# Moving one block sum and one group of quarter sums in a seven-product matmul's VectorE queue

## The chip, the cores and the metric

The kernel runs on one core of a Trainium2 chip. The metric is the device time of one execution in microseconds (us): 1536.24 us is the median of three runs of the kernel before (1536.0 to 1539.86). The engines are TensorE (PE; its weight loads are shown as PEld), VectorE (DVE), ScalarE (ACT), GpSimd (POOL) and SyncE (SP). SP, ACT and POOL issue the DMAs; here SP and ACT issue plain ones, and POOL those that also round float32 to float16.

## The reference

```python
def reference(a, b, alpha):          # a, b: 4096 x 4096 float32, alpha: 0.01
    x = np.matmul(a, b)
    return np.where(x > 0, x, alpha * x)
```

## The kernel before

The output is made in regions of 1024 x 1024, in four groups of four: a group `g` has 1024 rows of A, a region of it one set of 1024 columns of B. The very first region is computed plainly; the list `regions` holds the other fifteen. Each of these is a product of 2 x 2 blocks (A by 2 x 2 blocks of 512 rows and 2048 of K, B by 2 x 2 blocks of 2048 of K and 512 columns), and it is made with seven block products in place of eight. Every block of A or B is held as two units `k` of eight chunks of 128. All operands are float16, the accumulators are eight PSUM banks.

The sums of A's blocks are s1 = a21 + a22, s2 = s1 - a11, s3 = a11 - a21 and s4 = a12 - s2; they are made once in a group. Those of B's blocks are made in every region, in place: t3 = b22 - b12 over b12, t2 = b11 + t3 over b11, b21 - t2 over b21, and last t1 = b22 - t2 over t2. The seven products, `product(0)` to `product(6)` (L792, L652), are called first to seventh here: a11 b11, a12 b21, s2 t2, s3 t3, s1 t1, a22 (b21 - t2) and s4 b22. A whole one is 64 matmuls of 512 columns.

From the second group on, some of these products are themselves split once more in the same manner, into 2 x 2 quarters and seven quarter products of 16 matmuls of 256 columns (`quarter_product`, L745). Such a product needs four quarter sums of its A operand (`sums_of_a`, L692, with the sums at L700 and a DMA that keeps each in DRAM at L701; or `sums_of_s3`, L724) and its quarters of B (`t3_of_b` L680, `sums_of_b` with t2, t4 and t1 at L686, L688 and L690). There are three sorts of regions in a group from the second on:

- The **first region** of a group (`first_of_group`). Its sixth and seventh products are in quarters (`sixth_in_quarters` L843, `seventh_in_quarters` L892). It makes the quarter sums of s4 and of a22 and keeps them in DRAM for the group's other regions. The sums of a22 are used at once by its sixth product; those of s4 are read back from DRAM by ACT's queue during the sixth product (L860).
- The **second and third regions**, and in the last group the fourth too (`in_fourth`): the fourth product is in quarters as well (`fourth_in_quarters` L817). There are seven such regions.
- The **turning region**, the last one of a group but the final one, in which the next group's A is brought in. The change does not reach it.

The order of work is written out by hand: every engine runs its instructions in the order of the program, and only semaphores hold it back. So a place in the code is a place in the engine's queue. What stands in DVE's queue around the change, before:

1. In a first region, beside the third product (s2 t2): the adds of the second product's banks (L967), two leaky ReLUs (L312), b21 - t2 for two units (L588, called at L1084), the four quarter sums of s4 (L700, called at L1091), then t1 for two units (L588, called at L1109), the four quarter sums of a22 (L700, called at L1114), t3, t2, t4 and t1 of the sixth product's quarters of B (L680 to L690), t3 of the seventh's (L680), `add_v` (L972), and then the adds of the sixth product (L967 and, in `more`, L856). The sixth product's quarter products take turns on four PSUM banks: its fourth one and its sixth one add into a bank that DVE must have read before.
2. In an `in_fourth` region, beside the third product: t3, t2 and t4 of the fourth product's quarters, b21 - t2 for two units (L1084), t1 of the fourth product's quarters (L690, called at L1103), t1 of B's blocks for two units (L1109), then the adds of the fourth product's parts (L1124). The fourth product needs its t1 for its sixth quarter product.

Two buffer pools matter. `a16` has three buffers; each call of `new_a16` (L762) takes the next, and the first instruction that writes it waits until the last reader of its former content is done, a DMA out of it included. `x` has three large ones; its tile `q` (`t`, L1100) has four quarters and takes the place of s2, which is free when the third product has been issued and read. The rooms of the quarter sums before: s4's four in four `a16` buffers, a22's first three in three more, a22's fourth in `t[:, 3]`. The quarters `t[:, 0]` to `t[:, 2]` are used by the sixth product's sums of B (L1134).

`keep_x21` (L714) sends a quarter of the A operand itself to DRAM on SP's queue. POOL's queue fetches the next region's B with `fetch_b` (L507, the DMAs at L532): 512 KB each, four of them for each block, and each waits until the products have read the buffer that it fills.

Of the kernel before, what the change touches and what calls it, by code (L numbers as in the profile page):

```python
# [16 lines left out]
SUB = mybir.AluOpType.subtract  # L17
# [30 lines left out]
def kernel(  # L48
# [292 lines left out]
    for what, i, *more in order:  # L341
        if what == "a":
            r, tiles = more
            k = slice(r * rw, (r + 1) * rw)
# [106 lines left out]
    for i in range(1, len(steps)):  # L451
        t, h, u, first, last = steps[i]
# [19 lines left out]
        t, h, u, first, last = steps[i]  # L472
# [93 lines left out]
    def sum_a(g, name):  # L566
        blk = lambda h, half, k: at[g, h, 2 * half + k]
        if name != "s3" and (g, name, 0) not in s:
            new_s(g, name)
        for k in range(2):  # L570
            if name == "s1":
                a_sum(s[g, "s1", k], blk(1, 0, k), blk(1, 1, k), ADD)
            elif name == "s2":
                a_sum(s[g, "s2", k], s[g, "s1", k], blk(0, 0, k), SUB)
            elif name == "s3":
                s[g, "s3", k] = blk(1, 0, k)
                a_sum(s[g, "s3", k], blk(0, 0, k), blk(1, 0, k), SUB)
            else:
                a_sum(s[g, "s4", k], blk(0, 1, k), s[g, "s2", k], SUB)
# [6 lines left out]
    def b_sum(to, x0, x1, op):  # L586
        f = lambda t: t.rearrange("p c n -> p (c n)")
        nc.vector.tensor_tensor(f(to), f(x0), f(x1), op)  # L588
# [79 lines left out]
    def b_quarter(t):  # L668
        return t.rearrange("p (c n) -> p c n", n=HALF)

    def quarters_of_b(i, half, nt):
        return {(k, n): have_b[i, 2 * half + k, nt][:, :, n * HALF:(n + 1) * HALF]
                for k in range(2) for n in range(2)}

    def quarters_of_a(g, name):
        return {(h, k): operand(g, name, k)[:, :, h * HALF:(h + 1) * HALF, :] for h in range(2) for k in range(2)}
# [5 lines left out]
    def sums_of_b(y, to, some=(2, 4, 1)):  # L682
        tt = nc.vector.tensor_tensor
        f = lambda n: b_quarter(to[n])
        if 2 in some:
            tt(f(2), y[0, 1], y[0, 0], ADD)  # L686
        if 4 in some:
            tt(f(4), y[1, 0], f(2), SUB)  # L688
        if 1 in some:
            tt(f(1), y[1, 1], f(2), SUB)  # L690

    def sums_of_a(g, name, room):  # L692

        x = {key: q.rearrange("p c m e -> p c (m e)") for key, q in quarters_of_a(g, name).items()}
        made = {}

        def make(n, x0, x1, op):
            made[n] = room(n)
            f = lambda t: made[t].rearrange("p (c m) -> p c m", m=2 * HALF) if isinstance(t, int) else x[t]
            nc.vector.tensor_tensor(f(n), f(x0), f(x1), op)  # L700
            nc.sync.dma_start(kept_q[name][n - 1], made[n])  # L701

        make(1, (1, 0), (1, 1), ADD)
        make(2, 1, (0, 0), SUB)
        make(3, (0, 0), (1, 0), SUB)
        make(4, (0, 1), 2, SUB)

    def x21(g, name):
        return operand(g, name, 0)[:, :, HALF:, :]

    def by_chunk(t):
        return t.rearrange("p c m e -> p c (m e)") if len(t.shape) == 4 else t.rearrange("p (c m) -> p c m", m=2 * HALF)

    def keep_x21(g, name):  # L714
        if g < G - 1:
            nc.sync.dma_start(by_chunk(kept_x21[name]), by_chunk(x21(g, name)))
# [45 lines left out]
    def new_a16(_=None):  # L762
        return a16_pool.tile([P, QUARTER], DT, name="q16", tag="a16")
# [18 lines left out]
    for i, (g, j) in enumerate(regions):  # L782

        ks = (1, 0) if in_quarters else (0, 1)
# [3 lines left out]
        B = lambda half, nt, k: have_b[i, 2 * half + k, nt]  # L788
# [204 lines left out]
        def fetch_a(h, half, n):  # L993
            if n == 0:
                coming["rows", h, half] = small_pool.tile([P, 16], FP32, name="rows", tag=f"rows{half}")
            coming[h, half][n][0]()
# [21 lines left out]
        first_of_group = i == 0 or regions[i - 1][0] != g  # L1018
        in_quarters = g > 0 and not turning
        in_fourth = in_quarters and not first_of_group  # L1020
# [15 lines left out]
        if have_t2:  # L1036
            for k in ks:
                t = have_b[i, k, 0] = b_pool.tile([P, KC, NT], DT, name="b", tag="b11")
# [41 lines left out]
                    nc.sync.dma_start(kept_last[k, nt], B(1, nt, k).rearrange("p c n -> p (c n)"))  # L1080
        if i == 0:
            sum_a(g, "s4")
        for k in ks:
            b_sum(B(1, 0, k), B(1, 0, k), B(0, 0, k), SUB)  # L1084
        if turning and g:
            t3_of_b(quarters_of_b(i, 0, 1))
            for n in range(3):
                fetch_a(0, 1, n)
        if first_of_group and g:
            keep_x21(g, "s4")  # L1090
            sums_of_a(g, "s4", new_a16)  # L1091
        if not g:
            bring_a(0, 1)

# [4 lines left out]
        if g:  # L1099
            t = x_pool.tile([P, 4, QUARTER], DT, name="q", tag="x")  # L1100
        if in_fourth:
            tq[1] = t[:, 3]
            sums_of_b(quarters_of_b(i, 0, 1), tq, (1,))  # L1103
        elif turning and g:
            tq, sx4 = {2: t[:, 0], 4: t[:, 1], 1: t[:, 2]}, t[:, 3]
            sums_of_b(quarters_of_b(i, 0, 1), tq, (2, 4, 1))
            nc.sync.dma_start(sx4, kept_s3)
        for k in ks:
            b_sum(B(0, 0, k), B(1, 1, k), B(0, 0, k), SUB)  # L1109
        if late_ones:  # L1110
            late_ones[0].end()
        if in_quarters and first_of_group:
            sq = {4: t[:, 3]}
            sums_of_a(g, "a22", lambda n: sq.setdefault(n, sq[4] if n == 4 else new_a16()))  # L1114
            keep_x21(g, "a22")
# [106 lines left out]
    with tc.If(even == 0):  # L1222
        for m in range(M // RM):
            a_blocks = []
            for u in range(KU):
                t = a_pool.tile([P, KC // 2, RM, 2], BF16, name="a", tag=f"a{u // 2 + 1}{m % 2 + 1}")
# [6 lines left out]
            for n in range(N // NT):  # L1233
                banks = [new_bank(n % 2 * 4 + mt) for mt in range(MT)]
                cols = slice(n * NT, (n + 1) * NT)
                for u in range(KU):
                    t = b_pool.tile([P, KC, NT], BF16, name="b", tag=f"b{u // 2 + 1}{n % 2 + 1}")
# [8 lines left out]
                for mt in range(MT):  # L1246
                    t = c_pool.tile([P, 2, NT], FP32, name="c", tag=f"c{side}")[:, 0]
# [44 lines left out]
```

## Time and profile before

| what | value |
|---|---|
| median of three runs | 1536.24 us |
| the profiled execution's own time | 1538.0 us |
| its span, first to last instruction | 1535.8 us |
| PE busy | 1523.6 us (99% of the span) |
| DVE busy | 1158.6 us (75%) |
| ACT, POOL busy | 426.2 us (28%), 281.8 us (18%) |
| granted TensorE clock, mean | 0.999 |
| HBM | 361.76 MB read, 106.43 MB written |

The page names for each group of instructions the line, the engine, the tiles written and read, the count, the busy time, the mean of one in ns, and the idle time before them with what ended it. The timeline lists the instructions of an engine in order of time: start, length, line, operation, tiles, count and, in brackets, the idle time before and who ended it. A DMA is listed where it is issued; its time to landing runs from there to the last of its semaphore's updates. Matmuls are pipelined, so a row of 64 whole ones is shown as 13.98 us, while the next row starts 13.81 us after it; 16 quarter ones are shown as 1.91 us and follow each other by 1.75 us.

The first regions of groups two, three and four span about 411 to 508, 787 to 880 and 1160 to 1253 us; the seven `in_fourth` regions follow them.

### The profile page before, as it was taken

What the parts mean: (1) busy time and instruction counts of PE and PEld (TensorE: products, weight loads), DVE (VectorE), ACT (ScalarE), POOL (GpSimd) and SP (SyncE); (2) the same over time, 40 slices, a digit from 0 to 9 for tenths busy, and PEclk for the clock granted to TensorE, in tenths of its full rate; (3) what the DMA queues carried; (4) which work ended last, traced back from release to release, by engine and by line L of the source; (5) the groups of instructions that cost most, each with busy time, mean ns of one, the idle gap of its engine ahead of it and who ended that gap; (6) DMA issues with size and microseconds to landing.
All of it is one profiled execution on the core that took longest, in us unless ns stands there. A gap on an engine that the chain in (4) does not pass through costs nothing. (4 is left out here: it accounts for less than half of the span.)

```text
span 1535.8 us, 21827 instructions
## 1 busy us (share of the span) xinstructions
PE 1523.6 (99%) x8667; PEld 846.6 (55%) x8667; DVE 1158.6 (75%) x1207; ACT 426.2 (28%) x730; POOL 281.8 (18%) x458
## 2 busy tenths in 40 slices
PE   9999999999999999999999999999999999999998
PEld 4444444444445567574544747557554475746656
DVE  4368867765698686768769798686976968788497
ACT  2201344646310312103551031312464103041220
POOL 5641110143202011022220201110331110101100
PEclk9999999999999999999999999999999999999999
DMA  9999895998879979599798989959899895948934
GB/s 243 186 215 205 235 279 172 180 194 174 226 281 276 259 171 273 135 290 263 163 269 276 289 190 204 277 148 327 169 231 286 238 280 143 275 169 193 279 128 140
DMA packets 205442, 342.87 MB, mean 223 GB/s; under 512 B 18833, under 2 KB 148113, under 8 KB 195346
## 3 DMA queue, kind: packets, MB, share of 16 engines
q0 software_dynamic: 136704, 129.00, 52.7%
q1 hardware_dynamic: 62002, 186.81, 33.1%
q10 hardware_dynamic: 6624, 25.56, 4.4%
q8 instruction: 70, 1.15, 0.3%
q14 instruction: 42, 0.34, 0.1%
HBM read 361.76 MB, written 106.43 MB: 305 GB/s over the span
## 5 line engine op out<-in xcount | busy, mean ns | idle before, releaser
L801 PE MATMUL ps<-b,a 128*128 128x512 f16 x2624 | 570.9, 379 | 0.1
L801 PE MATMUL ps<-b,s 128*128 128x512 f16 x2240 | 489.2, 379 | 1.0 <-ACT c L814 1.0
L801 PEld LDWEIGHTS <-a 128*128 128x128 f16 x2624 | 256.8, 98 | 308.1 <-issue 0.6
L801 PEld LDWEIGHTS <-s 128*128 128x128 f16 x2240 | 219.0, 98 | 263.8 <-DVE b L588 1.5
L588 DVE TENSOR_TENSOR b<-b 128x4096 f16<-128x4096 f16 x104 | 235.1, 2289 | 66.7 <-DMA b<-in_b_dram 62.1
L532 POOL DMA_DIRECT2D b<-in_b_dram x160 | 118.5, 746 | 862.2 <-PE ps L751 325.2
L814 ACT COPY c<-ps 128x512 f32<-128x512 f32 x164 | 84.6, 596 | 444.9 <-PE ps L801 401.1
L141 DVE STREAM_TRANSPOSE a<-a 128x512 uint32<-128x512 uint32 (+2 forms) x120 | 127.0, 1106 | 101.4 <-DMA a<-in_a_dram 101.2
L132 POOL DMA_DIRECT2D a<-in_a_dram x252 | 137.3, 551 | 267.9 <-ACT junk L607 101.4
L751 PEld LDWEIGHTS <-q 128*128 128x128 f16 x1424 | 139.3, 98 | 17.8 <-issue 1.7
L607 ACT ACTIVATE junk<-a 128x512 bf16<-128x512 f16 x192 | 121.1, 631 | 99.6 <-DMA a<-in_a_dram 94.4
L312 DVE SCALAR_TENSOR_TENSOR c<-c 128x1024 f32<-128x1024 f32 (+2 forms) x123 | 141.8, 1195 | 3.9 <-ACT c L814 3.7
L230 ACT ACTIVATE sq<-b 128x2048 bf16<-128x2048 f16 x64 | 119.2, 1910 | 59.5 <-DVE sq L239 42.0
L751 PEld LDWEIGHTS <-a 128*128 128x128 f16 x1200 | 117.3, 98 | 18.7 <-DVE q L690 1.1
L967 DVE TENSOR_TENSOR c<-ps,c 128x512 f32<-128x512 f32 x140 | 87.5, 683 | 43.6 <-PE ps L801 42.0
L282 PE MATMUL ps<-b,a 128*128 128x512 f16 x512 | 112.4, 379 | 0.7 <-ACT a L379 0.2
L751 PE MATMUL ps<-b,q 128*128 128x256 f16 x784 | 91.9, 273 | 1.0 <-DVE c L856 1.0
L751 PE MATMUL ps<-b,a 128*128 128x256 f16 x752 | 88.3, 273 | 0.0
L282 PEld LDWEIGHTS <-a 128*128 128x128 f16 x512 | 49.6, 98 | 61.3 <-issue 1.7
L903 ACT COPY c<-ps 128x512 f32<-128x512 f32 x9 | 5.3, 586 | 272.0 <-PE ps L751 120.2
L751 PEld LDWEIGHTS <-s 128*128 128x128 f16 x624 | 61.1, 98 | 7.1
L856 DVE TENSOR_TENSOR c<-ps,c 128x512 f32<-128x512 f32 x80 | 52.3, 686 | 13.7 <-PE ps L751 13.7
(104 smaller groups left out, 903.7 us busy)
## 6 DMA issues: line engine op xcount, KB each, us to landing
b<-in_b_dram POOLq DMA_DIRECT2D x168, 512.0 KB, 13.9
out_dram<-c SPq DMA_DIRECT2D x240, 256.0 KB, 5.8
a<-in_a_dram POOLq DMA_DIRECT2D x244, 128.0 KB, 5.7
b<-kept SPq DMA_DIRECT2D x20, 1024.0 KB, 9.3
q<-kept_qs ACTq DMA_DIRECT2D x40, 512.0 KB, 7.9
s<-kept_s SPq DMA_DIRECT2D x18, 1024.0 KB, 7.4
q<-kept_qa SPq DMA_DIRECT2D x28, 512.0 KB, 7.5
b<-kept_last SPq DMA_DIRECT2D x12, 1024.0 KB, 11.5
```

Source lines behind the costliest of these rows:

```text
L132: nc.gpsimd.dma_start(a16[32 * q:32 * q + 32], src.rearrange("(g i) w -> i g w", i=32))
L141: nc.vector.transpose(part.rearrange("p c m e -> p c (m e)").bitcast(U32) .rearrange("p c (g i) -> p g c i", i=32), src[:, :, i * n:(i + 1 ...
L230: nc.scalar.activation(to, self.parts[n], SQUARE)
L282: nc.tensor.matmul(ps, a_cols(at[0, h, u], c, mt, (h, u) == (0, 0)), bt[0, u, nt][:, c, :], start=first, stop=last,)
L312: nc.vector.scalar_tensor_tensor(t, t, alpha, t, op0=MULT, op1=MAX if alpha <= 1 else MIN)
L532: nc.gpsimd.dma_start(t[:, c:c + 4, :], b_rows(j, u, c, 4, nt, g > 0))
L588: nc.vector.tensor_tensor(f(to), f(x0), f(x1), op)
L607: nc.scalar.activation(junk, piece[:, q, :], SQUARE, accum_out=to[:, 4 * n + q:4 * n + q + 1])
L751: nc.tensor.matmul(to[m], xq[:, c // 2, rows, c % 2], yq[:, c, :], start=first and c == 0 and m < banks, stop=c == KC - 1, skip_group_chec ...
L801: nc.tensor.matmul(banks[mt], a_cols(t, c, mt, t is first_a), B(half, nt, k)[:, c, :], start=first and (k, c) == todo[0], stop=(k, c) == t ...
L814: nc.scalar.copy(kept[mt], banks[mt])
L967: nc.vector.tensor_add(to, bank, to)
```

## The change

In the seven `in_fourth` regions, only the first unit of b21 - t2 stays in its place; the second is issued behind t1 of the fourth product's quarters. In the three first regions, the keeping of s4's quarter and the four quarter sums of s4 are issued behind t1 of B's blocks, directly ahead of a22's quarter sums, and the rooms change: s4's first three sums go to `t[:, 0]` to `t[:, 2]`, its fourth to an `a16` buffer. The number of instructions and of DMAs stays the same.

```diff
         if i == 0:
             sum_a(g, "s4")
-        for k in ks:
+        for k in ks[:1] if in_fourth else ks:
             b_sum(B(1, 0, k), B(1, 0, k), B(0, 0, k), SUB)
         if turning and g:
             t3_of_b(quarters_of_b(i, 0, 1))
             for n in range(3):
                 fetch_a(0, 1, n)
-        if first_of_group and g:
-            keep_x21(g, "s4")
-            sums_of_a(g, "s4", new_a16)
         if not g:
             bring_a(0, 1)
...
         if in_fourth:
             tq[1] = t[:, 3]
             sums_of_b(quarters_of_b(i, 0, 1), tq, (1,))
+            b_sum(B(1, 0, ks[1]), B(1, 0, ks[1]), B(0, 0, ks[1]), SUB)
         elif turning and g:
...
         if in_quarters and first_of_group:
+            keep_x21(g, "s4")
+            sums_of_a(g, "s4", lambda n: t[:, n - 1] if n < 4 else new_a16())
             sq = {4: t[:, 3]}
             sums_of_a(g, "a22", lambda n: sq.setdefault(n, sq[4] if n == 4 else new_a16()))
             keep_x21(g, "a22")
```

## The prediction

> **What bounds the kernel.** I read the list of waits first, for PE, since the page gives PE 1523.6 us busy of 1535.8 and a granted clock of 0.999: what a reordering can win lies in the 12.2 us between the two, and only where PE waits. Three of its seven rows lie near the change:
>
> ```profile
> PE ps L751 <- DVE c L856: 1.3, 2, 1.0
> PE ps L801 <- ACT c L814: 1.0, 1, 1.0
> PE ps L751 <- DVE q L690: 0.8, 1, 0.8
> ```
>
> (line, waited for: us in total, times, longest.) PE's timeline gives the places of these four waits. Three waits are in group two's first region: ahead of the fifth product, and ahead of the fourth and the sixth quarter product of the sixth.
>
> ```profile
> 467.99 13.99 PE L801 MATMUL ps<-b,s 128*128 128x512 f16 x64 [0.99 <-ACT c L814]
> ...
> 487.57 1.91 PE L751 MATMUL ps<-q,q 128*128 128x256 f16 x16 [0.36 <-DVE c L856]
> ...
> 492.23 1.91 PE L751 MATMUL ps<-b,q 128*128 128x256 f16 x16 [0.96 <-DVE c L856]
> ```
>
> One more, 0.78 us at 1304.56, is in group four's second region. The first regions of groups three and four have none. The ACT copy named at 467.99 is not what PE needs there: the weight loads' row names DVE b L588 for 1.5 us, and that is t1.
>
> Then DVE's timeline in that region, around the change:
>
> ```profile
> 459.43 1.23 DVE L700 TENSOR_TENSOR q<-s 128x2048 f16<-128x2048 f16 x1
> 460.69 1.23 DVE L700 TENSOR_TENSOR q<-q,s 128x2048 f16<-128x2048 f16 x1
> 461.83 1.22 DVE L700 TENSOR_TENSOR q<-s 128x2048 f16<-128x2048 f16 x1
> 464.50 1.23 DVE L700 TENSOR_TENSOR q<-s,q 128x2048 f16<-128x2048 f16 x1 [1.45 <-DMA kept_qs<-q]
> 465.64 4.49 DVE L588 TENSOR_TENSOR b<-b 128x4096 f16<-128x4096 f16 x2
> 471.14 1.23 DVE L700 TENSOR_TENSOR q<-a,a 128x2048 f16<-128x2048 f16 x1 [1.01 <-DMA kept_qs<-q]
> 473.14 1.23 DVE L700 TENSOR_TENSOR q<-q,a 128x2048 f16<-128x2048 f16 x1 [0.78 <-DMA kept_qs<-q]
> 475.17 1.22 DVE L700 TENSOR_TENSOR q<-a 128x2048 f16<-128x2048 f16 x1 [0.80 <-DMA kept_qs<-q]
> 476.31 1.22 DVE L700 TENSOR_TENSOR q<-a,q 128x2048 f16<-128x2048 f16 x1
> ```
>
> The reader is to see two things: t1 (L588) stands behind s4's four sums, and four of the eight quarter sums wait, 4.04 us together, until an `a16` buffer has left for DRAM. From 475.17 on DVE works without a gap until 492.18, and PE's two waits in the sixth product hang on that chain. So in this region DVE is the bound.
>
> **Part two, the `in_fourth` regions.** One L588 unit (2.29 us busy, 2.2 us from start to start) moves behind L690. In group four's second region:
>
> ```profile
> 1298.88 4.49 DVE L588 TENSOR_TENSOR b<-b 128x4096 f16<-128x4096 f16 x2
> 1303.28 1.22 DVE L690 TENSOR_TENSOR q<-b,q 128x2048 f16<-128x2048 f16 x1
> ...
> 1304.56 1.92 PE L751 MATMUL ps<-q,a 128*128 128x256 f16 x16 [0.78 <-DVE q L690]
> ```
>
> The quarter product before began at 1301.87, so PE could have begun this one at 1301.87 + 1.75 = 1303.62; it lost 0.94 us. L690 now starts at 1301.1 and ends at 1302.3: the wait goes, **-0.94**. What is late next is t1 of B's blocks, whose place in the queue does not change: its first unit ends at about 1306.7 and the fifth product would come at 1308.07 - 0.94 = 1307.13. It holds, by 0.4 us. In two other regions (641.52 and 1014.13) L690 waits until PE has read s2, for 1.38 and 0.62 us, and the moved unit now stands behind that wait: t1 ends up to 2.2 us later, at 649.3 and 1021.9. The fifth product reads its second unit from about 660.5 and 1033.1, so this is hidden by the rest of the fourth product; without that cover it would be 2 us each. In the other four nothing waits. Nothing here issues a DMA.
>
> **Part one, the three first regions.** It adds no instruction. It moves t1 by four sums ahead (465.64 to 459.43 in group two), so the stall at 467.99 goes: 467.99 against 453.01 + 13.81 = 466.82, that is 1.17 us. It takes three of s4's sums out of `a16`, so six small waits go (4.04 us here, and 0.37 and 0.42 us in groups three and four). SP's queue holds the same DMAs in the same order, since nothing of it lies between the two places.
>
> But it adds one wait. `a16` has three buffers. s4's fourth sum takes one, a22's first and second the others, and a22's third needs the one of s4's fourth, which must have **landed** in DRAM. Before, t1 (4.4 us) and two more sums lay between the two; now only two sums, 2.3 us. Behind the waiting sum all of DVE's queue stands: a22's fourth, the sixth product's t3, t2, t4, t1, `add_v`, and the adds that let PE go on. So the cost hangs on L, the time from the issue of that write to its landing.
>
> DVE's new times, by the row pitches above (two L588 4.40, four quarter sums 3.54 from first start to last, the last 1.23 long):
>
> - Group two: t1 459.43, s4's sums from 463.83, the fourth ends 468.60.
> - Group three: from the row of b21 - t2 at 826.72: t1 831.12, s4 835.52, the fourth ends 840.29.
> - Group four: from 1199.47: t1 1203.87, s4 1208.27, the fourth ends 1213.04.
>
> a22's third sum then starts at that end + L. From its start to PE's sixth quarter product the gapless chain takes 492.23 - 475.17 = 17.06 us. PE by itself, without any wait, would reach that quarter product at 466.82 + 13.81 + 5 x 1.745 = 489.36 in group two; in groups three and four it reached it at 862.98 + 1.745 = 864.73 and 1235.98 + 1.745 = 1237.73. So:
>
> - Group two: change = 468.60 + L + 17.06 - 492.23 = L - 6.57, not below 489.36 - 492.23 = -2.87.
> - Group three: 840.29 + L + 17.06 - 864.73 = L - 7.38, not below 0.
> - Group four: 1213.04 + L + 17.06 - 1237.73 = L - 7.63, not below 0.
>
> **What L is.** The trace has these very writes (512 KB, 128 x 4 KB) at other places; DMA to landing, least, median and most: s4's four in groups two and three, a22's four in groups three and four.
>
> ```profile
> DMA to landing us min/median/max: 3.7/9.1/10.0
> ...
> DMA to landing us min/median/max: 2.6/2.8/5.6
> ...
> DMA to landing us min/median/max: 8.5/9.3/10.3
> ...
> DMA to landing us min/median/max: 6.0/6.6/10.0
> ```
>
> Alone a write takes 2.6 to 2.8 us. Beside POOL's loads of the next region's B, which begin at 460.38, 835.73 and 1208.73, the last of four in a row takes 9.4 to 10.3 (in groups three and four that is a22's last, issued 3.5 us after the first); only where sums were themselves held up and came 1.1 to 2.0 us apart (a22 in group two) was it 6.1 to 7.0. Before, three of s4's four writes in groups three and four were out ahead of the loads, and none now is (first issues about 465.1, 836.8, 1209.5). Bounds: 3.7 (a first write beside a load) and 10.3. I take 9.5 in groups three and four, where the writes stand to the loads as s4's did in group two before (10.0 the third, 9.4 the fourth, by the sum that waited for it), and 8.2 in group two, between its own two rows, since there the first two loads have run 4.6 us by then.
>
> The Trainium skill (DMA: Bandwidth & Descriptors, "Queues, rings and completion order") says that each DMA engine takes turns between queues packet by packet. From 468 to 473 us SP's queue moved 340 packets and POOL's 356, so the trace agrees; by that alone four writes of 128 packets at 68 a us take 7.5 us from their first packet, L would be near 7, and the sum about -0.5 us.
>
> **Sum:** 8.2 - 6.57 = +1.6, 9.5 - 7.38 = +2.1, 9.5 - 7.63 = +1.9, and -0.9 from part two: **+4.7 us**. All four are on PE's path, since PE has no other wait after them that could swallow them. At both ends of L: 3.7 gives -2.9 - 0.9 = -3.8, and 10.3 gives 3.7 + 2.9 + 2.7 - 0.9 = +8.4. The sum is made against the span of 1535.8 us; the profiled execution took 1538.0, 2.2 us of it outside the span, and the median of the runs is 0.4 above the span. I add to the median: 1536.24 + 4.7 = **1540.9 us**.
>
> **Rivals.**
>
> 1. *Not slower: the writes land soon enough.* One mechanism: the end of s4's fourth write. It decides at L = 7.4: there the sum is +0.8 + 0 + 0 - 0.9, about zero. For it: a22's 6.1 to 7.0 in group two, and s4's fourth in groups three and four, 5.6 and 4.8, partly beside a load. Against: the 9.4 to 10.3 of every write that was last of four beside loads. At L = 6 it gives -0.6 - 0.9 = -1.5, 1534.7 us; at best -3.8, 1532.5 us. The Trainium skill (same page, "Anatomy of one DMA") gives 2.0 us + bytes / 436e3, that is an estimate of 3.2 us for 512 KB. By that this rival would hold, at its best; the rows alone agree with it, those beside loads do not.
> 2. *Slower still: the loads pay too.* The writes leave a stretch of idle DMA engines (before the loads begin) for a full one, so each write moved costs the loads behind it about 1.3 us. In group two's second region t2's first unit is ready at 534.79 for a third product at 535.58, 0.8 us of room. With L at 10.3 and one such miss of 1 us: +9.4, 1545.6 us. Against it: PE itself comes later by then.
> 3. *The change doesn't do what it says.* If L690 was not what PE waited for at 1304.56, part two gives nothing: +5.6, 1541.8 us. PE starts 0.1 us after its end, which speaks against this.
>
> **How the numbers follow.** About 0.3% (4.6 us) is what a measurement of this kernel can tell from no change. Forecast (L of 8 to 10, +1.4 to +7.5): 0.6; rival one 0.25; rival two 0.1; rival three 0.05. Of the forecast a little over half lies above 4.6 us, so slower is 0.32 + 0.1 + 0.04 = 0.46; faster would need more than the -3.8 of the best end, 0.03; the rest, 0.51, is within. The range leaves out the best end of rival one and the last of rival two: 1534.7 to 1545.
>
> **What would show it.** In the changed trace: no wait at the fifth product in group two and none at L690 in group four's second region; of the six small waits of L700 one left in each first region, on `kept_qs`, of L - 2.3, some 6 to 7 us, at a22's third sum; DVE c L856 ahead of the sixth product's fourth and sixth quarter products in all three first regions. L below 7 in the rows of these writes, or a22's third sum in another buffer, would make the forecast wrong.

## The result and the profile after

| | before | after |
|---|---|---|
| median of 22 runs each | 1536.05 us | 1543.12 us |
| lowest and highest | 1533.49 to 1541.61 | 1539.87 to 1546.64 |
| profiled execution, own time | 1538.0 | 1542.66 |
| its span | 1535.8 | 1540.8 |
| ratio of the times | | 1.0048, 95% interval 1.0041 to 1.0055 |

The change makes the kernel slower by 7.1 us by the medians. The two profiled executions differ by 5.0 us of span; the one of before lies 2.0 us above its median, the one of after 0.5 us below, which makes up most of the rest. What follows about places is read from these 5.0 us.

PE's rows of the list of waits of the changed kernel (line, waited for: us in total, times, longest):

```profile
PE ps L751 <- DVE c L856: 5.0, 4, 1.5
PE ps L751 <- DVE q L690: 2.3, 1, 2.3
...
PE ps L801 <- DVE b L588: 0.4, 1, 0.4
PE ps L801 <- DMA b<-in_b_dram: 0.4, 1, 0.4
PE ps L751 <- DVE q L734: 0.4, 1, 0.4
```

The 1.0 us at the fifth product is gone. The adds of the sixth product (L856) cost 5.0 us in place of 1.3, and the 2.3 us on L690 is a new wait at another place than the old 0.8. DVE's timeline of the changed kernel in group two's first region shows where they come from:

```profile
463.01 1.22 DVE L700 TENSOR_TENSOR q<-s 128x2048 f16<-128x2048 f16 x1
...
466.54 1.22 DVE L700 TENSOR_TENSOR q<-s,q 128x2048 f16<-128x2048 f16 x1
467.68 1.22 DVE L700 TENSOR_TENSOR q<-a,a 128x2048 f16<-128x2048 f16 x1
468.93 1.23 DVE L700 TENSOR_TENSOR q<-q,a 128x2048 f16<-128x2048 f16 x1
476.73 1.23 DVE L700 TENSOR_TENSOR q<-a 128x2048 f16<-128x2048 f16 x1 [6.58 <-DMA kept_qs<-q]
```

The small waits between the sums are gone, and one large one stands ahead of a22's third sum, until s4's fourth write has landed. Groups three and four have the same wait, of 6.36 and 8.05 us. Behind it PE is late. PE's timeline of the changed kernel, group two and then group four:

```profile
465.87 13.98 PE L801 MATMUL ps<-b,s 128*128 128x512 f16 x64
...
483.94 1.92 PE L751 MATMUL ps<-q,q 128*128 128x256 f16 x16 [2.35 <-DVE q L690]
...
489.13 1.91 PE L751 MATMUL ps<-q,q 128*128 128x256 f16 x16 [1.53 <-DVE c L856]
...
493.80 1.91 PE L751 MATMUL ps<-b,q 128*128 128x256 f16 x16 [0.96 <-DVE c L856]
...
1238.34 1.91 PE L751 MATMUL ps<-q,q 128*128 128x256 f16 x16 [1.53 <-DVE c L856]
...
1243.01 1.91 PE L751 MATMUL ps<-b,q 128*128 128x256 f16 x16 [0.96 <-DVE c L856]
```

The fifth product begins at 465.87 in place of 467.99, and the sixth quarter product at 493.80 in place of 492.23, so a lead of 2.1 us is lost again, with 1.6 on top. Of this lead 1.2 us is the stall that is gone, and 0.95 us was there already at the product ahead of it (452.06 in place of 453.01), which the change does not touch. In group four the sixth quarter product comes at 1243.01 in place of 1237.73. Followed instruction by instruction, PE's lag behind the kernel before goes like this:

| stretch | change of PE's lag |
|---|---|
| start of the kernel, not touched by the change | -0.9 |
| group two: 1.2 won at the fifth product, 3.7 lost in the sixth | +2.5 |
| group three, first region | 0 |
| group three, second region (two waits, one of them for a load) | +1.05 |
| group four, first region | +2.8 |
| group four, second region, a wait on L734 | +0.6 |
| there, t1 of the fourth product (part two) | -0.9 |
| small steps elsewhere | -0.1 |
| sum | +5.0 |

### The profile page after: what moved, and what is told of

It is laid out like the page before. It is cut to its first block, busy times and chain, and to the rows that moved or that the text cites. A ratio compares the mean times of both kernels' runs of the same rounds, so it can differ in the third digit from the quotient of the medians.

```text
span 1540.8 us, 21831 instructions
## 1 busy us (share of the span) xinstructions
PE 1523.7 (99%) x8667; PEld 846.6 (55%) x8667; DVE 1157.4 (75%) x1207; ACT 426.4 (28%) x730; POOL 281.9 (18%) x458
## 5 line engine op out<-in xcount | busy, mean ns | idle before, releaser
L588 DVE TENSOR_TENSOR b<-b 128x4096 f16<-128x4096 f16 x104 | 234.8, 2289 | 64.5 <-DMA b<-in_b_dram 60.7
L967 DVE TENSOR_TENSOR c<-ps,c 128x512 f32<-128x512 f32 x140 | 87.5, 682 | 37.9 <-PE ps L801 24.7
L751 PE MATMUL ps<-q,q 128*128 128x256 f16 x480 | 57.3, 273 | 5.4 <-DVE c L856 3.1
```

The lines of the kernel that those rows point to most:

```text
L751: nc.tensor.matmul(to[m], xq[:, c // 2, rows, c % 2], yq[:, c, :], start=first and c == 0 and m < banks, stop=c == KC - 1, skip_group_chec ...
L967: nc.vector.tensor_add(to, bank, to)
```

## The experiments

Each kernel was run beside the kernel before on the same chip; ratios are against it. The experiments were run in three batches on three chips, so kernels of different batches are compared by their ratios.

**The two parts alone.** In the first kernel part two is undone, in the second part one.

```diff
-        for k in ks[:1] if in_fourth else ks:        # part1_alone
+        for k in ks:
-            b_sum(B(1, 0, ks[1]), B(1, 0, ks[1]), B(0, 0, ks[1]), SUB)
```

> Part one without part two (the second unit of b21 - t2 back ahead of t1 of the fourth product's quarters). The theory (the wait of a22's third sum for the write of s4's fourth costs the time; part two takes away one stall of 0.94 us): the changed kernel's +7.1 plus 0.9, some +8.0 us against the kernel before, and the stall ahead of the quarter product that needs L690 in group four's second region is back. The rival that part two is what costs: about 0 to -1 us.

> Part two without part one (s4's quarter sums back ahead of t1, in four a16 buffers). The theory: -0.9 us against the kernel before, with no wait of PE in group four's second region, and t1 of B's blocks some 2.2 us later in two regions without anyone waiting for it. The rival that part two costs or does nothing: 0 or above.

Part one alone: 1543.68 us, ratio 1.0066 (1.0053 to 1.0079). Part two alone: 1534.24 us, 0.9997 (0.9988 to 1.0006). The loss is all in part one. Part two wins its 0.99 us at the quarter product behind L690 in the trace of its own kernel, but no difference shows in the time.

This trace shows one thing more. Up to group two's first region the kernel of part two alone has the same instructions as the kernel before, and yet the stalls that the prediction read there are not in it. PE's timeline, from the product ahead of the fifth to the next region, with every wait of that stretch:

```profile
454.50 13.98 PE L801 MATMUL ps<-b,a 128*128 128x512 f16 x64
468.31 13.98 PE L801 MATMUL ps<-b,s 128*128 128x512 f16 x64
...
508.95 26.06 PE L801 MATMUL ps<-b,a 128*128 128x512 f16 x120 [0.48 <-DMA b<-in_b_dram]
```

PE came 1.5 us later to 454.50 than in the kernel before, by differences in the first 95 us, and DVE's sums waited 1.8 us for their buffers in place of 4.0. Of the three stalls in the profiled execution of before, 2.9 us together, none is left. So how much PE stalls there differs from one execution to the next by as much as the change could win there.

**The wait taken away.** In this kernel, early_room, a22's third sum gets an `a16` buffer that held s4's first sum, not its fourth.

```diff
-            sums_of_a(g, "s4", lambda n: t[:, n - 1] if n < 4 else new_a16())
+            sums_of_a(g, "s4", lambda n: new_a16() if n == 1 else t[:, {2: 0, 3: 2, 4: 1}[n]])
```

> The changed kernel with one edit: of s4's quarter sums the first takes the a16 buffer, and the second, third and fourth take t's quarters 0, 2 and 1. a22's third sum then waits for the write of s4's first sum, issued 3.5 us earlier and ahead of three others. All instructions and DMAs stay where they are. The theory (the wait on the buffer sets the time): the wait falls from 6.4 to 8.1 us to 0 in groups two and three and to 2.3 or less in group four, and PE's waits in the sixth products go: -2.9 in group two and 0 in group four, less 0.9 by part two, plus up to 2 us of late loads in group three's second region: -1 to -4 us against the kernel before. The rival (the writes, moved beside POOL's loads, cost the time by making those late): it moves the same writes, so it stays at +4 or more.

It came out at 1544.92 us, ratio 1.0076 (1.0063 to 1.0089): slower than before by 10 us, and not faster by 1 to 4. The wait did go, as DVE's timeline of this kernel shows:

```profile
468.82 1.22 DVE L700 TENSOR_TENSOR q<-q,a 128x2048 f16<-128x2048 f16 x1
469.96 1.22 DVE L700 TENSOR_TENSOR q<-a 128x2048 f16<-128x2048 f16 x1
```

PE reaches the sixth quarter product of group two's sixth product at 488.45, 3.8 us ahead of the kernel before; 0.9 of this is from the start of the kernel. Then PE waits for something else. The waits of this kernel, and PE's timeline in the next region:

```profile
PE ps L801 <- DMA b<-in_b_dram: 6.5, 3, 3.8
PE ps L751 <- DVE q L734: 2.1, 1, 2.1
```

```profile
505.70 1.89 PE L801 MATMUL ps<-b,a 128*128 128x512 f16 x8 [1.36 <-DMA b<-in_b_dram]
511.35 4.87 PE L801 MATMUL ps<-b,a 128*128 128x512 f16 x14 [3.77 <-DMA b<-in_b_dram]
```

The 3.8 us in hand turn into a lag of 1.7 us, and of 3.4 by the next product (538.94 in place of 535.58; see the last section). Waits of 0.6 to 1.0 us for writes of s4, ahead of single sums of B's quarters, are left in DVE's queue. So the theory that the wait of a22's third sum is all that the change costs, and that without it the change wins, falls.

**Another order with a shorter wait.** s4's and a22's quarter sums are made 1, 2, 4, 3 (`make(4)` ahead of `make(3)` in `sums_of_a`; sums_1243).

> The changed kernel with one edit: in both groups of quarter sums the fourth is made ahead of the third, so that the write of s4's fourth is issued one sum earlier and two more sums lie between it and a22's third, which is now the last. Buffers stay as in the changed kernel. The theory: DVE's chain behind the wait comes some 3 us earlier (1.1 by the sum that is now made ahead of the wait, about 2 by a write that is third in the row and not fourth), so group two loses 2.5 - 3 and group four 2.8 - 3, at least zero: about +1 to +3 us against the kernel before. The rival (late loads): +7 as the changed kernel.

It took 1549.41 us in four runs, ratio 1.0098 (1.0083 to 1.0112), the slowest of all, and outside both expectations. DVE's waits for the quarter sums' buffers in the three first regions fell from 21.0 us to 9.4 in all. PE has no wait in the sixth products to speak of, and again waits for the loads:

```profile
PE ps L801 <- DMA b<-in_b_dram: 7.6, 4, 3.5
PE ps L751 <- DVE q L734: 2.1, 1, 2.1
```

So a new theory: the cost is the place of s4's writes, in the stretch in which POOL brings the next region's B and the DMA engines have little to spare (in the trace of before the profile gives them a busy share of 0.45 from 450 to 460 us, and of 1.13 from 470 to 480). Either DVE waits for the writes, or, if DVE does not, the writes of s4 and a22 go out together and the loads come late. In group two's first region the traces have, for the load that PE waits for in early_room:

| kernel | s4's fourth write issued | that load issued | landed | PE waited for it |
|---|---|---|---|---|
| before | 465.75 | 483.00 | 508.59 | 0 |
| after | 467.79 | 480.88 | 504.30 | 0 |
| early_room | 467.68 | 480.91 | 511.31 | 3.8 |
| s4_first (below) | 460.97 | 482.62 | 504.92 | 0 |

In the kernel before, PE took that load's data at 509.68, so it had 1.1 us of room. In the changed kernel DVE's wait held a22's last writes back by 7 us, and the load came 7 us earlier than without the wait.

**The writes moved the other way.** If this holds, s4's sums must go ahead, not back. Part two is kept, s4's four sums go to `a16` buffers again (the pool still has three), and s4's block moves ahead of b21 - t2 (s4_first); in the second kernel (s4_first_units) b21 - t2 and t1 also alternate, unit by unit.

```diff
+        if first_of_group and g:
+            keep_x21(g, "s4")
+            sums_of_a(g, "s4", new_a16)
         for k in ks[:1] if in_fourth else ks:
             b_sum(B(1, 0, k), B(1, 0, k), B(0, 0, k), SUB)
...
-        if first_of_group and g:
-            keep_x21(g, "s4")
-            sums_of_a(g, "s4", new_a16)
```

> Part two kept; in first regions s4's quarter sums go the other way, ahead of b21 - t2, so 4.4 us earlier than in the kernel before, in their four a16 buffers; t1 stays where it was. The new theory (what costs is that s4's writes run beside POOL's loads of the next region's B; taking the wait on the buffer away only hands the loss on to the loads): the writes are out before or just as the loads begin, the waits of the quarter sums on buffers go in all groups, and so do the 1.3 us of PE's waits in group two's sixth product; the stall of 1.2 us ahead of the fifth product stays, since t1 is where it was. With part two's 0.9: about -2 us against the kernel before. A rival (any change of this order costs, by t1 or by DVE's queue): 0 or above.

> As the run before, and in first regions b21 - t2 and t1 go unit by unit: b21 - t2 and t1 of the first unit, then both of the second, so t1's first unit ends some 4.4 us sooner than in the kernel before. No DMA changes its place by it. The new theory: the stall ahead of the fifth product goes too; group two wins 2.9 us at most (PE without any wait) if the loads of the next region keep up, 1.1 us of room plus what they gain by the writes' earlier place: -2.5 to -3.8 us with part two. If the loads are what then comes last: about -2.

Measured 1534.13 us, ratio 0.9995 (0.9986 to 1.0004), and 1533.78 us, 0.9998 (0.9989 to 1.0007): by the ratios some 8 us faster than the changed kernel, and no difference to the kernel before that can be told. The forecast gains of 2 and of 2.5 to 3.8 us did not come. These are all of PE's waits in the trace of s4_first, and all lie in the first region or ahead of it, where neither part reaches:

```profile
PE wp L105 <- DVE x L91: 1.2, 1, 1.2
PE ps L282 <- DVE a L141: 1.1, 1, 1.1
PE turned L372 <- DVE a_rounded L356: 0.3, 1, 0.3
```

The span is 1532.3 us, 3.5 below that of before, while the medians differ by 0.1. Two signs of the first expectation missed as well. The stall ahead of the fifth product, which was to stay, is gone. The waits of the sums for their buffers, which were to go, stay in all three groups (2.42, 2.92 and 0.92 us ahead of s4's fourth sum), and no wait of PE follows them:

```profile
459.71 1.23 DVE L700 TENSOR_TENSOR q<-s,q 128x2048 f16<-128x2048 f16 x1 [2.42 <-DMA kept_qs<-q]
```

So the direction of the theory holds and my size does not. The waits in the profiled execution of before were no measure of what its other executions lose; part two alone, above, shows one that loses none of them.

**Less to write.** These two kernels write only half of each quarter sum in groups three and four (so those groups' later regions read buffers in DRAM that are half filled); the edit is put on early_room (early_half) and on the changed kernel (after_half).

```diff
-            nc.sync.dma_start(kept_q[name][n - 1], made[n])
+            wide = QUARTER // 2 if g > 1 else QUARTER
+            nc.sync.dma_start(kept_q[name][n - 1][:, :wide], made[n][:, :wide])
```

> The kernel with s4's first sum in the a16 buffer (early_room, +10.2 us against the kernel before), and in groups three and four only one half of each quarter sum is written to DRAM (the other half of what is read back is then group two's). That leaves out 2 MB of writes in each of these first regions, and nothing in group two. The new theory: with the writes halved the loads of B are in time again, so the 1.6 us at group three's second region and the 2.3 us in group four's second go, while group two's loss stays as it was: about +6 us against the kernel before. A rival (the late loads there come from PE's or POOL's order, not from the bytes of the writes): +10, as without the halving.

> The changed kernel, and in groups three and four only one half of each quarter sum is written to DRAM. The new theory: the write that a22's third sum waits for lands sooner (some 5 to 7 us after its issue, not 8.7 and 10.4), so the 2.8 us of PE's waits in group four's sixth product go, and the 1.0 and 0.6 us of late loads too; group two's +2.5 stays: about +2.5 to +3 us against the kernel before. A rival (the wait is DVE's own order): +7.

On early_room: 1539.42 us, ratio 1.0034 (1.0022 to 1.0046), half the loss. The late loads are gone from groups three and four and stay in group two, where nothing was halved. On the changed kernel: 1537.87 us, 1.0024 (1.0015 to 1.0033), also half. There the wait in group four falls from 8.05 to 5.79 us and the loss in its sixth product from 2.8 to 0.7:

```profile
1222.02 1.22 DVE L700 TENSOR_TENSOR q<-a 128x2048 f16<-128x2048 f16 x1 [5.79 <-DMA kept_qs<-q]
```

Both forms of the loss go with the bytes written, which is what the theory asks for.

**Rooms and places apart.** The first kernel has part two and the new rooms, with s4's sums where they were, ahead of t1. The second has the changed order with the old rooms, all four of s4's sums in `a16`. The third has part one in group two alone.

> Part two and the new rooms of the change, but the old order: s4's quarter sums ahead of t1 of B's blocks (three in t, the fourth in an a16 buffer). The new theory (the loss comes from the place of s4's writes beside POOL's loads, that is from the order): no loss; the write that a22's third sum waits for has t1 and two sums to land, so the waits of sums on buffers go or shrink to some 2 us in group two: -0.5 to -2 us against the kernel before. The rival (the loss comes from the rooms: four waits put into one): +5 or more, as the changed kernel.

> The change with the old rooms: s4's quarter sums behind t1 of B's blocks as in the changed kernel, but all four in a16 buffers. The new theory: the writes stand where the changed kernel has them, so the loss stays and grows, since s4's fourth and a22's first three sums now wait in turn for the writes of s4's first to fourth, the last of them issued later: +8 to +12 us against the kernel before. The rival (the loss comes from the new rooms): about 0.

> Part two, and part one in group two alone; groups three and four as before. By the traces group two's move costs 2.5 us net (its t1 stall of 1.2 us is gone in this) and the rest of the loss lies in groups three and four: +1 to +2.5 us against the kernel before. If the move pays where t1 was late and costs only elsewhere: below 0.

| kernel | us | before beside it | ratio (interval) |
|---|---|---|---|
| rooms_alone | 1533.84 | 1535.23 | 0.9991 (0.9982 to 1.0) |
| rooms_as_before | 1546.25 | 1535.23 | 1.0062 (1.0049 to 1.0076) |
| moved_g2_only | 1537.43 | 1535.23 | 1.0012 (1.0003 to 1.0021) |

The new rooms cost nothing by themselves: a22's third sum then waits 1.93 us in group two, since t1 lies between. The order costs its full price with either rooms. Group two alone gives 1.8 us of the loss (0.5 to 3.2 by the interval). The sum has 0.7 for this kernel, 1.6 with 0.9 off for part two; its trace shows +1.2 for group two, where the changed kernel's has +2.5.

One line of rooms_alone does not fit the theory that late loads come from the new place alone. PE's timeline:

```profile
509.66 27.75 PE L801 MATMUL ps<-b,a 128*128 128x512 f16 x120 [2.91 <-DMA b<-in_b_dram]
```

Here s4's writes are at the old place, and the load still landed only at 509.62. PE had come 3.1 us early, without a stall in the region, and so it waited for the load that the profiled execution of before needed at 509.68. This was the slowest of the kernel's eleven runs (1537.99 us, the lowest 1532.63). So a load can be the next limit at the old place too; what the new place adds is shown by the times of the kernels, not by the presence of such a wait.

No kernel was shown to beat the kernel before; the three with s4's sums at the old place or ahead of it (s4_first, s4_first_units, rooms_alone) cannot be told from it, and by the ratios they beat the changed one by some 8 us. The point estimates, 0.05 to 0.09%, would need many more runs.

## Why the prediction was right, and where its sizes were off

- **The wait and what hangs on it: right.** I forecast one wait of 6 to 7 us in each first region; it was 6.58, 6.36 and 8.05. The chain of 17.06 us from a22's third sum to the sixth quarter product holds to 0.01 us: 476.73 + 17.06 = 493.79 in group two (493.80), 1225.94 + 17.06 = 1243.00 in group four (1243.01). Of the signs that I named, the waits at the fifth product and on L690 in group four are gone, and one of the small waits is left in each first region, group four's above my 6 to 7 us. The waits on L856 came in groups two and four, not in group three, and I had not named the 2.35 us on L690 ahead of group two's second quarter product.
- **L: a little low.** Taken 8.2, 9.5 and 9.5; measured about 8.9 (issued 467.79, the sum released at 476.7), 8.7 (840.14 to 848.84) and 10.4 (1215.52 to 1225.91). With these the formulas give +2.3 in group two and +2.8 in group four; PE's lag grew by 2.5 and 2.8.
- **Group three's +2.1: wrong, it was 0.** The step that failed is the adding up of the three regions: "All four are on PE's path, since PE has no other wait after them that could swallow them." What could swallow one was the lag that PE had by then. In group three DVE was not held by PE there: s4's sums started at 835.35, where I had 835.52, while PE came to the sixth product 1.56 us later than before. a22's third sum at 848.87 + 17.06 = 865.93 is ahead of PE's own 864.73 + 1.56 = 866.29. So what group two had lost paid for group three. The kernel of part one alone shows the other case: there group two cost PE only 0.75 us, PE came to group three's sixth product with no lag (-0.1 us), and group three cost 2.4 us, near the 2.1 that I had:

```profile
867.00 1.91 PE L751 MATMUL ps<-b,q 128*128 128x256 f16 x16 [0.96 <-DVE c L856]
```

  In group four DVE came later along with PE (the write issued at 1215.52, I had the sum end at 1213.04), and the loss was added.
- **The loads: in no sum of mine, +1.6 us.** This is rival two, which I tied to L of 10.3 and held up against "PE itself comes later by then". It came at L of 8.7. Of the 1.6 us, 0.6 is a direct wait for a load and 0.5 one behind L588, both in group three's second region, and 0.6 stands behind L734 in group four's. PE's timeline of the changed kernel in the first of these:

```profile
884.30 26.06 PE L801 MATMUL ps<-b,a 128*128 128x512 f16 x120 [0.40 <-DMA b<-in_b_dram]
910.79 1.45 PE L801 MATMUL ps<-b,s 128*128 128x512 f16 x6 [0.43 <-DVE b L588]
```

  The load was issued at 858.75 and landed 25.5 us later, at 884.25; before, it was issued at 857.18 and took 21.3. In group four the wait on L734 is, as I read it, the same thing one step on: DVE had stood for a load. This last link is argued, since in the kernel before DVE stood there for 12.05 us too, and the load took 25.0 us there and 26.1 here.

```profile
1279.13 2.29 DVE L588 TENSOR_TENSOR b<-b 128x4096 f16<-128x4096 f16 x1 [13.10 <-DMA b<-in_b_dram]
```

- **Part two's -0.9: right in the trace**, and its cover as well (the two delays at 641 and 1014 us cost nothing). The quarter product is at 1309.46 against 1304.56, a lag of 4.90 where it was 5.84 one quarter product earlier:

```profile
1304.21 1.92 PE L751 MATMUL ps<-b,q 128*128 128x256 f16 x16 [0.39 <-DVE q L734]
...
1309.46 1.91 PE L751 MATMUL ps<-q,a 128*128 128x256 f16 x16
```

- **Rival one: no.** Its point was L of 7.4; s4's fourth writes in the changed kernel took 8.7 to 10.4. The estimate by packets, L near 7, was too low as well. The Trainium skill's fit (DMA: Bandwidth & Descriptors, "Anatomy of one DMA": about 2.0 us and bytes / 436e3, an estimate of 3.2 us for these 512 KB) is near what such a write took alone, 2.6 to 2.8 us, and far from the 8.7 to 10.4 here; it was measured, by the page, for one DMA on another path.
- **The best end, L = 3.7 and -3.8 us: wrong as a price.** I let the time fall as far as DVE alone allows. early_room, which has no wait ahead of a22's third sum, shows that the loads hold it: PE comes to the next region early, the load comes 2.7 us later than in the kernel before (511.31 and 508.59), and the lead is lost with more. What the sum lacked is the next limit behind DVE's queue, the DMA engines; rival two had it, with a chance of 0.1.
- **The size in time.** My sum was against one execution, 4.7, where spans give 5.0 and medians 7.1. That 4.7 lies so near 5.0 is in part luck: group three's +2.1 did not come, the larger losses in groups two and four (5.3 in place of 3.5) and the loads' 1.6 did, and 0.9 us was won at the start of the kernel, where the change does nothing. An execution without the stalls of before's profiled one is seen in part two alone. Whether most executions of before are like it stays open, since only one of them has a trace; if they are, the changed kernel has less to win than I took, which would fit the larger 7.1. Why SP's writes begin so late beside the loads stays open too.

## What to carry to other kernels

Before a write is moved, look at what the DMA engines carry at its new place, not only at who waits for it. Here the writes moved beside the loads cost time either as a wait for the buffer or as late loads, and taking the wait away only changed the form. Waits in one profile are not a sum of savings: each has the next limit behind it (here 1.1 us of room at a load), and a wait in one region may pay for one in the next. Here the writes at their old place, or issued earlier still, avoided the loss; no kernel was shown to gain on the one before.

## What the runs showed of the hardware

**A wait of PE can cost more than its length.** In early_room, after the 3.77 us wait, the granted clock is half for 3.4 us. Its stretches (us, busy of PE, PEld, DVE, ACT and POOL, granted clock, DMA share, GB/s):

```profile
511.90:515.30 3.40, 3.40 (x10) 1.21 (x8) 1.45 (x2) 3.40 (x3) 0.43 (x1) 0.50 1.16 267
515.40:518.00 2.60, 2.60 (x13) 1.18 (x12) 2.03 (x2) 1.44 (x1) 0.00 (x0) 1.00 1.15 283
```

About eight matmuls come every 0.43 us in place of 0.216, which is the 1.7 us between the lags of 1.7 and 3.4 there. Such a stretch of 3.4 us followed waits of 2.91 to 3.77 us in early_room, early_half, rooms_alone, rooms_as_before (3.53) and sums_1243 (3.50), and a second one in sums_1243 a wait of only 2.15 us:

```profile
1309.44 3.27 PE L751 MATMUL ps<-b,q 128*128 128x256 f16 x16 [2.15 <-DVE q L734]
```

No such stretch followed a wait of 2.15 us in early_room, 2.35 in the changed kernel or 2.46 in sums_1243. So the length of the wait alone does not decide it. The Trainium skill (TensorE: Matmul & The Clock Gate, "What's actually happening") tells of a window of 3.4 us that runs freely and of a clock that is halved after an idle one; the length and the half agree with these rows, while here 2.15 us of wait was enough in one case.

**Queues that move as many packets need not move as many bytes.** From 468 to 473 us in before, SP's queue moved 340 packets with 1.26 MB and POOL's 356 with 0.36 MB: most of SP's hold 4 KB, most of POOL's 1 KB. That is some 250 KB a us for the writes and 70 for the loads. It is not a rule for every stretch: from 841.5 to 845.6 us in before it was 104 packets of SP's beside 656 of POOL's, although the first of a22's writes on SP's queue was issued at 841.90. That the loads come late because of this share is argued, not shown; that they come earlier with fewer bytes to write is what early_half shows for groups three and four.
